# Moving roots, weight splits and a turn in a hybrid encoder trunk

## The chip, the cores and the metric

The kernel runs on one core of one Trainium2 chip. The metric is the device time of one execution in microseconds (us). The engines are named as in the profile: PE is TensorE (matrix products; PEld loads its weights), DVE is VectorE, ACT is ScalarE, POOL is GpSimd, SP issues DMAs.

## The reference

Two token batches (512 and 256 tokens, width 1024, float32) go through a trunk of two layers with shared weights. Each layer is a feed-forward network, a token mixer and a second feed-forward network, each on a normalised input and added to the residual stream:

```python
for li in range(DEPTH):                      # DEPTH = 2
    x = x + 0.5 * swiglu_ffn(rmsnorm(x, norm_g[li, 0]), ffn_w1[li, 0], ffn_w2[li, 0])
    h = rmsnorm(x, norm_g[li, 1])
    mix = hgrn2_mixer(h, ...) if li % 3 == 0 else window_gqa_mixer(h, ...)
    x = x + mix
    x = x + 0.5 * swiglu_ffn(rmsnorm(x, norm_g[li, 2]), ffn_w1[li, 1], ffn_w2[li, 1])
return rmsnorm(x, final_norm_g)
```

The first mixer is a gated linear recurrence in both directions with 8 heads: `f = lb + (1 - lb) * sigmoid(...)` are the gates, the outputs are normalised per head by `rsqrt(mean(o * o) + eps)` and multiplied by `silu(g)`. The second is attention with 16 query heads in 4 groups over a window of 128 tokens on each side, with a rotary turn of 16 of 64 columns, a sink logit per head and a softmax; its output goes through `w_o`.

## The kernel before

Every large product is made of float32 operands that are split in two: a high part (a cast, on ACT) and a low part (the rest, a subtraction on DVE). Three matmuls then replace one: high by high, high by low, low by high (lines 286 to 288, and 524 and 605 in the feed-forward networks, where a seven-product scheme saves one product in eight). Weights come by DMA into four raw buffers, are cast by line 186 and rested by line 187 (227 and 228 in the feed-forward networks) into eight tiles named `w`, in the order of a queue that is planned at the start; a next tile is staged when an earlier one is done with. The 768 tokens stand in six blocks of 128, three to each half.

A feed-forward network ends with six blocks: two residual additions each (line 668), then `after_block`. That normalises the block (`norm_block`: square with its sum on line 344, root on 345, reciprocal on 346, scale on 349). With the third block of a half it defers two "turns": each turn transposes four of the eight 128-column pieces of the half's three blocks on TensorE (line 409), copies them scaled to the high part (416, ACT) and makes the low part (417, DVE). Deferred steps are taken one by one with `run_later`, at places that the loops name. At a mixer both turns of the first half are taken during blocks 4 and 5, those of the second half inside the mixer's first projection, on whose later blocks they bear.

The recurrence projects three outputs per head (a copy and two sigmoids, line 831) and weaves this with the scan of an earlier head. A scan's sections write scores (line 850), multiply running products (943 to 951), copy operands (894, 896), carry a state over the blocks (982, 985) and form the output (998). The sums of squares of the heads' outputs (`hss`) become roots and reciprocals (`hrs`, lines 1066 and 1067) in two batches of four heads; the projection of `g` then uses Silu and multiplies with these (1097 and 1103). ACT has to load a table (ACT_TABLE_LOAD in the profile) when a function of another set is next.

Attention is a pipeline over 24 units of a block and a group. A unit's scores (1383) go through a maximum (1399), exponentials (1412), a sum and its reciprocal (1424, 1425) and a scaling (1428); its weights are transposed (1435), copied (1437) and multiplied with the values (1444). Between units stand pieces of the query projections, whose results are rotated (1158 to 1165), turned (1369) and split (291, 292), and later pieces of the output projection.

The order in which each engine executes is fixed at build time by a scheduling layer that weighs readiness; `issue_after(x)` makes an instruction stand behind instruction `x` in it. Line numbers in the profile are those of the code below; in the changed file they are 2 to 7 higher.

Of the kernel before, what the change touches and what calls it, by code (L numbers as in the profile page):

```python
# [9 lines left out]
F32 = mybir.dt.float32  # L10
# [3 lines left out]
ALU = mybir.AluOpType  # L14
# [35 lines left out]
class Trunk:  # L50
# [125 lines left out]
    def plain_steps(self, key, raw, shape):  # L176
        self.plains += 1
        tiles = []

        def go(part=0, parts=1, eng=self.nc.vector):  # L180
            n = shape[0] * shape[1]
            if not part:
                tiles[:] = [self.wtile()[:, :n].rearrange("p (a b) -> p a b", a=shape[0]) for _ in range(2)]
            ks = slice(part * shape[0] // parts, (part + 1) * shape[0] // parts)
            hi, lo = (t[:, ks, :] for t in tiles)
            self.nc.scalar.copy(hi, raw[:, ks, :])  # L186
            eng.tensor_sub(lo, raw[:, ks, :], hi.bitcast(F32))  # L187
            if part == parts - 1:
                self.staged[key] = (*tiles, 2)

        if self.plains == 1:
            return [(2, lambda: go(0, 2, self.nc.gpsimd)), (0, lambda: go(1, 2, self.nc.gpsimd))]
        if self.plains == 2:
            return [(2, lambda: [go(i, 2) for i in range(2)])]
        return [(2, go)]
# [260 lines left out]

    xn = [None] * NBLK
    normed = mixed = first = halved = None
    plains = 0

    def after_block(self, b, row):
# [208 lines left out]
    def ffn(self, tag, next_row):  # L670
# [59 lines left out]
        for b in range(NBLK):  # L730
            if next_row is None and b == NBLK - 1:
                self.last_block(b, lambda c: [add(b, k, hids[k], (c,)) for k in range(2)] and banks[(b, c)])
                return
            for i, k in (((0, 0), (1, 0), (0, 1)), ((1, 1),))[b] if b < 2 else ((b, 0), (b, 1)):
                add(i, k, hids[k])
            for c in range(2):
                self.added = self.add_x(self.x[b][:, c * 512 : (c + 1) * 512], banks[(b, c)], 0.5)
            self.after_block(b, next_row)
            if b >= 4:
                self.run_later()  # L740

    def spill_x(self):
# [71 lines left out]
    def hgrn_proj(self, h, out):  # L814
        nc = self.nc
        qk = self.big([P, 2, T])
        qs, kd = qk[:, 0, :], qk[:, 1, :]
        f, q, k = (self.big([P, 2, T]) for _ in range(3))
        for c0, dst, func in ((0, qs, AF.Copy), (3, f[:, 1, :], AF.Sigmoid), (4, f[:, 0, :], AF.Sigmoid)):
            key = ("hgrn", h, c0)  # L820
            wh, wl = self.take(key)
            for s, (off, n) in enumerate(SEQS):
                ps = self.ps(n)
                for kk in range(NC):
                    b = tuple(self.h[kk][:, i, off : off + n] for i in range(2))
                    self.mm3(ps, (wh[:, kk, :], wl[:, kk, :]), b, kk == 0, kk == NC - 1)
                    if kk in ((1, 3, 5), (3,))[s]:
                        yield
                if s:
                    self.done(key)  # L830
                nc.scalar.activation(dst[:, off : off + n], ps, func)
                yield
        for d in range(2):
            fd, j = f[:, 1 - d, :], slice(h, h + 1)
            nc.vector.tensor_scalar(fd, fd, self.om_lb[:, d, j], self.lb[:, d, j], ALU.mult, ALU.add)
            nc.scalar.activation(k[:, d, :], fd, AF.Identity, bias=1.0, scale=-1.0)
            nc.vector.tensor_mul(q[:, 1 - d, :], qs, fd)
        nc.vector.tensor_add(kd, k[:, 0, :], k[:, 1, :])
        out.update(h=h, qs=qs, kd=kd, f=f, q=q, k=k)
# [194 lines left out]
    def hgrn(self, lb_row, gn_row, next_row):  # L1034
        nc = self.nc
# [28 lines left out]
        def rstds(half):  # L1064
            r = rs[:, half * 4 : half * 4 + 4, :]
            nc.scalar.activation(r, self.hss[:, half * 4 : half * 4 + 4, :], AF.Sqrt, bias=self.eps, scale=1.0 / P)
            nc.vector.reciprocal(r, r)
# [22 lines left out]
        def put_g(half):  # L1090
            us = {}

            def f(s, b, ps):
                if not half and not us:
                    rstds(0)
                sg = self.tmp(512)
                nc.scalar.activation(sg, ps, AF.Silu)
                off, n = SEQS[s]
# [252 lines left out]
class Unit:  # L1351
# [69 lines left out]
    def denominator(self):  # L1421
        nc = self.k.nc
        den, sk = self.den, self.sk
        nc.vector.tensor_add(den, den, sk)
        nc.vector.reciprocal(den, den)
        for i in range(GQ):
            p = self.sc[:, i, : self.nk]
            nc.vector.tensor_scalar(p, p, den[:, i : i + 1], 1.0, ALU.mult, ALU.mult)

    def probs(self, j):  # L1430
        k = self.k
# [140 lines left out]
```

## Time and profile before

| what | value |
| --- | --- |
| median of 3 runs | 2735.54 us (2735.27 to 2736.42) |
| profiled execution, its time | 2735.33 us |
| its span | 2733.5 us |
| PE busy | 2720.8 us |
| DVE busy | 2111.6 us |
| ACT busy | 1340.6 us |
| POOL busy | 205.0 us |

A row of the timeline gives the start in us from the span's start, the duration in us, the engine, the line, the operation, the tiles written and read, the shapes and a count of merged instructions; in brackets stands how long the engine had been idle before and what released it. Consecutive matmuls overlap: a 512-wide one is shown with 0.39 us, and the next starts 0.23 us after it.

### The profile page before, as it was taken

The numbers are of one execution on the slowest core, as the hardware profiler recorded it, in microseconds if no ns is written. First come the engines' busy times: TensorE is split into PE (matmuls) and PEld (weight loads), VectorE is DVE, ScalarE is ACT, GpSimd is POOL, SyncE is SP. The second block draws the span as 40 slices with busy tenths as digits, with TensorE's granted clock in tenths as the row PEclk, the third lists the DMA queues.
The fourth block names the chain that finished last, engine by engine and source line by source line (L and its number), as shares of the span: only waits on it lengthen the run. The fifth ranks groups of instructions, "written<-read, shape, count | busy, mean of one in ns | idle before, by whom it ended". The sixth has DMA issues, their size and how long they took to land.

```text
span 2733.5 us, 44559 instructions
## 1 busy us (share of the span) xinstructions
PE 2720.8 (100%) x17305; PEld 2483.1 (91%) x17305; DVE 2111.6 (77%) x3789; ACT 1340.6 (49%) x2508; POOL 205.0 (7%) x243
## 2 busy tenths in 40 slices
PE   9999999999999999999999999999999999999998
PEld 9999999889888889999999999999887789999998
DVE  8888788567476778878888878887847768787877
ACT  6444444456466554444446444444446754444444
POOL 1110110000000000011100011101000000111000
PEclk9999999999999999999999999999999999999999
DMA  6554554311110424455543355544512123555443
GB/s 183 137 125 115 127 145 117 123 55 48 55 41 25 141 68 113 120 147 128 128 121 102 89 128 139 135 116 113 147 58 78 47 62 84 133 139 133 118 112 108
DMA packets 331411, 293.98 MB, mean 108 GB/s; under 512 B 11752, under 2 KB 258240, under 8 KB 331200
## 3 DMA queue, kind: packets, MB, share of 16 engines
q1 hardware_dynamic: 294352, 212.89, 26.4%
q0 software_dynamic: 32544, 64.76, 13.3%
q10 hardware_dynamic: 4304, 13.49, 1.4%
q8 instruction: 135, 2.21, 0.3%
q14 instruction: 76, 0.62, 0.1%
HBM read 216.91 MB, written 9.44 MB: 83 GB/s over the span
## 4 chain that ended last, share of the span: by engine, by line
PE 96%; DVE 2%; ACT 1%; issue 0%; DMA 0%; DVEq 0%; SPq 0%; ACTq 0%
PE ps L524 43%; PE ps L605 21%; PE ps L286 8%; PE ps L288 8%; PE ps L287 8%; PE ps L850 1%; PE ps L640 1%; PE ps L998 1%; PE ps L1444 1%; PE ps L1435 1%; PE ps L1383 1%; PE ps L409 1%; PE ps L974 0%; DVE w L187 0%; PE ps L963 0%
## 5 line engine op out<-in xcount | busy, mean ns | idle before, releaser
L524 PE MATMUL ps<-big,w 128*128 128x384 f32 x6720 | 1169.4, 334 | 0.0
L524 PEld LDWEIGHTS ps<-big,w 128*128 128x128 f32 x6720 | 1165.9, 188 | 1.8 <-ACT tA L541 0.2
L227 ACT CAST w<-wr 128x512 fp32r<-128x512 f32 (+1 forms) x606 | 423.6, 710 | 737.7 <-DVE wr L241 327.2
L228 DVE TENSOR_TENSOR w<-wr,w 128x512 fp32r<-128x512 f32 (+1 forms) x606 | 481.2, 799 | 227.7 <-ACT w L227 158.6
L605 PE MATMUL ps<-w,big 128*128 128x512 f32 x2520 | 575.5, 389 | 0.0
L605 PEld LDWEIGHTS ps<-w,big 128*128 128x128 f32 x2520 | 472.6, 188 | 97.8 <-DVE x L668 0.4
L668 DVE SCALAR_TENSOR_TENSOR x<-ps,x 128x512 f32<-128x512 f32 x468 | 303.4, 683 | 8.0 <-PE ps L288 8.0
L286 PE MATMUL ps<-w,big 128*128 128x512 f32 x576 | 232.5, 404 | 0.3
L288 PE MATMUL ps<-w,big 128*128 128x512 f32 x576 | 225.6, 392 | 1.0 <-DVE big L417 1.0
L287 PE MATMUL ps<-w,big 128*128 128x512 f32 x576 | 225.1, 391 | 0.0
L286 PE MATMUL ps<-big,w 128*128 128x384 f32 (+2 forms) x640 | 218.0, 342 | 0.1
L287 PE MATMUL ps<-big,w 128*128 128x384 f32 (+2 forms) x640 | 215.8, 337 | 0.4 <-DVE big L369 0.2
L288 PE MATMUL ps<-big,w 128*128 128x384 f32 (+2 forms) x640 | 215.0, 336 | 0.0
L291 ACT CAST big<-tA 128x384 fp32r<-128x384 f32 x296 | 147.9, 512 | 118.6 <-DVE tA L569 40.4
L153 POOL DMA_DIRECT2D s<-wr x122 | 106.3, 913 | 1300.1 <-DMA wr<-in_ffn_w_dram 614.8
L187 DVE TENSOR_TENSOR w<-wr,w 128x1024 fp32r<-128x1024 f32 (+1 forms) x88 | 106.1, 1210 | 82.5 <-ACT w L186 73.9
L292 DVE TENSOR_TENSOR big<-tA,big 128x384 fp32r<-128x384 f32 x296 | 160.5, 553 | 7.4 <-ACT big L291 7.0
L153 POOL DMA_DIRECT2D wr<-wr x101 | 87.6, 867 | 1010.4 <-DVE tA L1103 387.1
L186 ACT CAST w<-wr 128x1024 fp32r<-128x1024 f32 (+1 forms) x90 | 93.0, 1036 | 91.9 <-PE ps L287 65.6
L286 PEld LDWEIGHTS ps<-w,big 128*128 128x128 f32 x576 | 108.3, 188 | 26.3 <-issue 5.3
L288 PEld LDWEIGHTS ps<-w,big 128*128 128x128 f32 x576 | 108.1, 188 | 25.1 <-DVE big L417 1.7
L287 PEld LDWEIGHTS ps<-big,w 128*128 128x128 f32 x640 | 121.0, 189 | 9.3 <-DVE big L292 1.0
(191 smaller groups left out, 2897.2 us busy)
## 6 DMA issues: line engine op xcount, KB each, us to landing
wr<-in_ffn_w_dram SPq DMA_DIRECT2D x264, 512.0 KB, 3.9
s<-wr POOLq DMA_DIRECT2D x122, 256.0 KB, 5.2
s<-in_ffn_w_dram SPq DMA_DIRECT2D x120, 256.0 KB, 3.3
wr<-wr POOLq DMA_DIRECT2D x80, 256.0 KB, 4.2
wr<-in_hg_w_in_dram SPq DMA_DIRECT2D x40, 512.0 KB, 3.9
wr<-wr POOLq DMA_DIRECT2D x21, 512.0 KB, 6.0
spill<-x ACTq DMA_DIRECT2D x12, 512.0 KB, 3.0
x<-spill ACTq DMA_DIRECT2D x12, 512.0 KB, 3.3
```

Source lines behind the costliest of these rows:

```text
L153: self.nc.gpsimd.dma_start(out, src, accum_op=ALU.add)
L187: eng.tensor_sub(lo, raw[:, ks, :], hi.bitcast(F32))
L227: nc.scalar.copy(h, src)
L228: low = nc.vector.tensor_sub(l, src, h.bitcast(F32)).ins
L286: nc.tensor.matmul(out, a[0], b[0], start=first, stop=False)
L287: nc.tensor.matmul(out, a[0], b[1], start=False, stop=False)
L288: nc.tensor.matmul(out, a[1], b[0], start=False, stop=last)
L291: self.nc.scalar.copy(hi, src)
L292: return self.nc.vector.tensor_sub(lo, src, hi.bitcast(F32)).ins
L524: self.nc.tensor.matmul(ps, a[x], b[y], start=first and k == 0 and i == 0, stop=k == 3 and i == 2, skip_group_check=True,)
L605: nc.tensor.matmul(ps, a[x], w[y], start=name == chain and kp == 0 and q == 0, stop=kp == 1 and q == 2, skip_group_check=True,)
L668: return self.nc.vector.scalar_tensor_tensor(x, ps, c, x, ALU.mult, ALU.add).ins
```

## The change

Three edits. The first batch of the recurrence's roots is ordered behind the last sigmoid: `self.gate` holds the latest sigmoid or copy of a head's projection when the first block of the `g` projection is recorded. The low parts of attention's output weights, all but the first tile's, are ordered behind the latest scaling of a unit that has been recorded (`self.normal`). And where a mixer follows, a deferred step is taken ahead of the norms of blocks 4 and 5 and not behind them.

```diff
@@ -184,7 +184,9 @@
             hi, lo = (t[:, ks, :] for t in tiles)
             self.nc.scalar.copy(hi, raw[:, ks, :])
-            eng.tensor_sub(lo, raw[:, ks, :], hi.bitcast(F32))
+            follow = self.normal if key[0] == "sw_o" and any(key[1:]) else None
+            with self.tc.issue_after(follow) if follow else nullcontext():
+                eng.tensor_sub(lo, raw[:, ks, :], hi.bitcast(F32))
@@ -456,6 +458,7 @@
     normed = mixed = first = halved = None
+    normal = None
@@ -735,8 +738,11 @@
                 self.added = self.add_x(self.x[b][:, c * 512 : (c + 1) * 512], banks[(b, c)], 0.5)
+            mixer = next_row is not None and next_row % 3 == 1
+            if b >= 4 and mixer:
+                self.run_later()
             self.after_block(b, next_row)
-            if b >= 4:
+            if b >= 4 and not mixer:
                 self.run_later()
@@ -828,7 +834,7 @@
-                nc.scalar.activation(dst[:, off : off + n], ps, func)
+                self.gate = nc.scalar.activation(dst[:, off : off + n], ps, func).ins
@@ -1092,7 +1098,8 @@
                 if not half and not us:
-                    rstds(0)
+                    with self.tc.issue_after(self.gate):
+                        rstds(0)
@@ -1425,7 +1432,7 @@
             p = self.sc[:, i, : self.nk]
-            nc.vector.tensor_scalar(p, p, den[:, i : i + 1], 1.0, ALU.mult, ALU.mult)
+            self.k.normal = nc.vector.tensor_scalar(p, p, den[:, i : i + 1], 1.0, ALU.mult, ALU.mult).ins
```

How the orders change, at the places of which the prediction speaks. First ACT, in the scans of head 3 (before) and head 7 (behind the last sigmoid; `big_8244` and `big_8595` are its scores and transposed keys). Before, in head 3:

```order
L894 COPY big_7296<-big_6444 128x768
L1066 ACT_TABLE_LOAD
L1066 ACTIVATE hrs<-hss,eps 128x24
L896 COPY big_6441<-big_6443 128x768
L894 COPY big_6441<-big_6444 128x768
L894 COPY big_7296<-big_6444 128x768
L831 ACT_TABLE_LOAD
L831 ACTIVATE big_7180<-ps_7353 128x512
```

And of the change, in head 7:

```order
L837 ACTIVATE big_8044<-ps_8478 128x256
L1072 ACT_TABLE_LOAD
L1072 ACTIVATE hrs<-hss,eps 128x24
L886 COPY big_8244<-ps_8542 64x6x64
L842 ACTIVATE big_8046<-big_8044 128x768
L886 COPY big_8244<-ps_8541 64x6x64 x2
L970 COPY big_8595<-ps_8596 128x512
L970 COPY big_8595<-ps_8602 128x512
L886 COPY big_8244<-ps_8542 64x6x64
L892 COPY big_8244<-big_8246 32x6x32 x4
L900 COPY big_8703<-big_8046 128x768
L1104 ACT_TABLE_LOAD
```

Both loads are gone from head 3; one load and the roots stand behind the last sigmoid, and one copy for the next scan has moved behind the four copies of scores.

Second DVE, at the first mixer's start (at the second it is alike): `w_4667` and `w_4676` are the low parts of the projection's third and fourth weight tiles. Before:

```order
L668 SCALAR_TENSOR_TENSOR x_131<-ps_4659,x_131 128x512
L346 RECIPROCAL stat_4618<-stat_4618 128x1
L417 SCALAR_TENSOR_TENSOR big_4623<-ps_4631,cols,big_4623 128x384
L349 TENSOR_SCALAR big_4617<-x_129,stat_4618 128x1024
L417 SCALAR_TENSOR_TENSOR big_4624<-ps_4637,cols,big_4624 128x384
L417 SCALAR_TENSOR_TENSOR big_4625<-ps_4643,cols,big_4625 128x384
L417 SCALAR_TENSOR_TENSOR big_4626<-ps_4649,cols,big_4626 128x384
L187 TENSOR_TENSOR w_4667<-wr_4407,w_4666 128x1024
L417 SCALAR_TENSOR_TENSOR big_4627<-ps_4689,cols,big_4627 128x384
L187 TENSOR_TENSOR w_4676<-wr_4439,w_4675 128x1024
L346 RECIPROCAL stat_4684<-stat_4684 128x1
L417 SCALAR_TENSOR_TENSOR big_4628<-ps_4695,cols,big_4628 128x384
```

Of the change:

```order
L419 SCALAR_TENSOR_TENSOR big_4620<-ps_4643,cols,big_4620 128x384
L671 SCALAR_TENSOR_TENSOR x_131<-ps_4655,x_131 128x512
L671 SCALAR_TENSOR_TENSOR x_131<-ps_4659,x_131 128x512
L348 RECIPROCAL stat_4650<-stat_4650 128x1
L189 TENSOR_TENSOR w_4667<-wr_4407,w_4666 128x1024
L351 TENSOR_SCALAR big_4649<-x_129,stat_4650 128x1024
L189 TENSOR_TENSOR w_4676<-wr_4439,w_4675 128x1024
L419 SCALAR_TENSOR_TENSOR big_4621<-ps_4683,cols,big_4621 128x384
L419 SCALAR_TENSOR_TENSOR big_4622<-ps_4689,cols,big_4622 128x384
L419 SCALAR_TENSOR_TENSOR big_4623<-ps_4695,cols,big_4623 128x384
L419 SCALAR_TENSOR_TENSOR big_4624<-ps_4701,cols,big_4624 128x384
L348 RECIPROCAL stat_4708<-stat_4708 128x1
```

The first turn's low parts (the last of four is the first row) now precede block 5's additions, and the second turn's four stand together behind both splits and ahead of block 5's reciprocal (the last row) and scale.

Third DVE, in attention at the first two of the output weights' late splits: `w_20580` and `w_20643` are their low parts, `big_20503` and `big_20591` two successive units' scores. Before:

```order
L1425 RECIPROCAL stat_20505<-stat_20505 128x4
L187 TENSOR_TENSOR w_20580<-wr_19627,w_20579 128x1024
L1428 TENSOR_SCALAR big_20503<-big_20503,stat_20505 128x384 x4
L292 TENSOR_TENSOR tA_20588<-ps_20585,tA_20588 128x256
L1399 ISA big_20591,stat_20592<-ps_20598,big_18930,nsinks 128x384
L1399 ISA stat_20592 128x1
L292 TENSOR_TENSOR big_20621<-ps_20599,big_20620 128x2x128
L1418 TENSOR_TENSOR stat_20594<-stat_20592,nsinks 128x4
L187 TENSOR_TENSOR w_20643<-wr_19646,w_20642 128x1024
```

Of the change:

```order
L1432 RECIPROCAL stat_20505<-stat_20505 128x4
L1406 ISA big_20591,stat_20592<-ps_20598,big_18930,nsinks 128x384
L1406 ISA stat_20592 128x1
L1435 TENSOR_SCALAR big_20503<-big_20503,stat_20505 128x384 x4
L189 TENSOR_TENSOR w_20580<-wr_19627,w_20579 128x1024
L294 TENSOR_TENSOR tA_20588<-ps_20585,tA_20588 128x256
L294 TENSOR_TENSOR big_20621<-ps_20599,big_20620 128x2x128
L1425 TENSOR_TENSOR stat_20594<-stat_20592,nsinks 128x4
```

The first late split has changed sides with the scaling and the fourth maximum, and the second has left this stretch: it stands behind the next unit's scaling, with the third right behind it. On PE the eight transposes that wait for the scaling, four of which stood between the first two matmuls of a group and four behind the second, now stand together ahead of that group.

## The prediction

> **What bounds the kernel now.** I read the page's busy shares and its chain first, then the list of what TensorE waited for, then the timeline at each such wait.
>
> ```profile
> span 2733.5 us, 44559 instructions
> PE 2720.8 (100%) x17305; PEld 2483.1 (91%) x17305; DVE 2111.6 (77%) x3789; ACT 1340.6 (49%) x2508; POOL 205.0 (7%) x243
> PE 96%; DVE 2%; ACT 1%; issue 0%; DMA 0%; DVEq 0%; SPq 0%; ACTq 0%
> ```
>
> TensorE (PE) is busy for 2720.8 of 2733.5 us and makes 96% of the chain that ended last. So whatever the change does to VectorE (DVE) and ScalarE (ACT), time can only come from moments at which TensorE itself stands still. Its list of waits is short. It counts from the modelled end of a matmul; the loss is read better from start to start. The first place is in the recurrence, head 3:
>
> ```profile
> 750.80 1.28 ACT L1066 ACT_TABLE_LOAD   x1
> 752.10 0.32 ACT L1066 ACTIVATE hrs<-hss,eps 128x24 f32<-128x24 f32 x1
> 755.32 0.39 PE L288 MATMUL ps<-big,w 128*128 128x512 f32 x1
> 756.03 1.28 ACT L831 ACT_TABLE_LOAD   x1
> 757.33 0.60 ACT L831 ACTIVATE big<-ps 128x512 f32<-128x512 f32 x1
> 757.82 0.83 ACT L896 COPY big<-big 128x768 f32<-128x768 f32 x1
> 758.68 0.96 DVE L951 TENSOR_TENSOR big<-big,big 128x768 f32<-128x768 f32 x1 [1.60 <-ACT big L896]
> 758.18 0.28 PE L287 MATMUL ps<-big,w 128*128 128x256 f32 x1
> 758.30 0.28 PE L288 MATMUL ps<-big,w 128*128 128x256 f32 x1
> 759.69 1.48 PE L850 MATMUL ps<-big,big 128*32 128x32 f32 x144 [1.11 <-DVE big L951]
> ```
>
> Matmuls of this width start every 0.12 us (758.18 to 758.30), and the next one starts 1.39 later: lost 1.27. The chain behind it is the table load for the sigmoid (756.03), the sigmoid, the copy L896, the product L951, the scores L850. The sigmoid's table has to be loaded again because the roots at 752.10 had put theirs in its place.
>
> The second and third are the first projections of the two mixers:
>
> ```profile
> 506.98 0.27 PE L409 MATMUL ps<-ident_r,big 128*128 128x128 f32 x1
> 507.75 0.50 PE L288 MATMUL ps<-w,big 128*128 128x512 f32 x1 [0.50 <-DVE big L417]
> 1980.93 0.27 PE L409 MATMUL ps<-ident_r,big 128*128 128x128 f32 x1
> 1981.66 0.50 PE L288 MATMUL ps<-w,big 128*128 128x512 f32 x1 [0.46 <-DVE big L417]
> ```
>
> A transpose takes 0.11 of TensorE's time (four in 0.45, 2132.04 to 2132.49 below), so 0.77 and 0.73 between these starts are losses of 0.66 and 0.62. The matmul waits for the low part of the turned input (L417), which on DVE stands behind a split of a weight tile (L187).
>
> The fourth and fifth are in attention, where the splits of the output weights begin:
>
> ```profile
> 2129.27 0.17 DVE L1425 RECIPROCAL stat<-stat 128x4 f32<-128x4 f32 x1
> 2129.59 1.23 DVE L187 TENSOR_TENSOR w<-wr,w 128x1024 fp32r<-128x1024 f32 x1
> 2130.73 1.40 DVE L1428 TENSOR_SCALAR big<-big,stat 128x384 f32<-128x384 f32 x4
> 2132.38 0.61 DVE L1399 CUSTOM_DVE_ANT_0 big<-ps,big,nsinks 128x384 f32<-128x384 f32 x1
> 2130.31 0.40 PE L286 MATMUL ps<-w,big 128*128 128x512 f32 x1
> 2131.29 0.68 PE L1435 MATMUL ps<-ident_r,big 128*128 128x128 f32 x4 [0.58 <-DVE big L1428]
> 2132.04 0.69 PE L1435 MATMUL ps<-ident_r,big 128*128 128x128 f32 x4
> 2132.49 0.48 PE L288 MATMUL ps<-w,big 128*128 128x512 f32 x1
> 2136.07 1.04 ACT L186 CAST w<-wr 128x1024 fp32r<-128x1024 f32 x1
> 2137.38 0.59 ACT L1437 COPY tA<-ps 128x512 f32<-128x512 f32 x1
> 2137.42 0.40 PE L288 MATMUL ps<-w,big 128*128 128x512 f32 x1
> 2138.02 0.65 PE L1444 MATMUL ps<-tA,big 128*64 128x256 f32 x4 [0.20 <-ACT tA L1437]
> ```
>
> A 512-wide matmul occupies TensorE for 0.23, so the transposes lose 0.98 - 0.23 = 0.75 to the split that stands ahead of L1428, and L1444 loses 0.60 - 0.23 = 0.37 to a copy that stands behind a cast. The five together are 1.27 + 0.66 + 0.62 + 0.75 + 0.37 = 3.67 us, 0.13% of the run: the ceiling of what this change can give.
>
> **The change part by part. Roots.** In the new order ACT has 18 table loads for 19 and none in head 3. The 512-wide product that the sigmoid reads ends at 755.32 + 0.39 = 755.7, so the sigmoid runs from about 755.75, not 757.33, the copy from 756.25 to 757.05 and L951 (0.96) to 758.05. TensorE is there at 758.42. The 1.27 goes, with 0.3 of cover.
>
> The load and the roots now stand in head 7, between the last sigmoid and the copies of the scores:
>
> ```profile
> 842.69 0.38 ACT L831 ACTIVATE big<-ps 128x256 f32<-128x256 f32 x1
> 844.15 0.96 ACT L880 COPY big<-ps 64x384 f32<-64x384 f32 x2 [1.09 <-PE ps L850]
> 853.50 1.12 DVE L985 SCALAR_TENSOR_TENSOR big<-big,big,ps 128x128 f32<-128x128 f32 x4
> 854.80 0.38 PE L998 MATMUL ps<-x,big 128*128 128x128 f32 x2
> ```
>
> ACT idles from 843.07 to 844.15. Load and roots take 1.62 together (750.80 to 752.42), with the usual overlap of 0.1 some 1.5, so L880 starts 0.45 late. From there ACT has no gap up to the Silu's load; the copies that the states need follow that, L985 follows these, and its end at 854.62 is 0.18 ahead of L998. There is no other cover: I take 0.35 lost, near the row's count, with bounds of 0 (the slack in these handovers swallows it) and 1.5 (none of the idle time serves). The reciprocal of the roots moves along to a place where DVE has time ahead of its users.
>
> By its neighbouring rows a load costs 1.30 on ACT: the roots start 0.02 after its end. The Trainium skill (ScalarE: Activation LUTs, What ACT_TABLE_LOAD costs) adds a drain of about 1.38 to each switch, 2.66 in all; by that the new place would lose 1.4 more and the time be 2734.1. This trace shows no such gap at these loads.
>
> **Mixers.** The first turn's four scaled copies (L416) and low parts (L417) now come ahead of the squares and scales of blocks 4 and 5, and the second turn's low parts stand in a row behind both splits. I lay the new order out with the rows' durations:
>
> ```profile
> 496.53 1.47 PE L409 MATMUL ps<-ident_r,big 128*128 128x128 f32 x12
> 498.71 0.56 ACT L416 ACTIVATE big<-ps,cols 128x384 fp32r<-128x384 f32 x1
> 500.75 1.06 ACT L186 CAST w<-wr 128x1024 fp32r<-128x1024 f32 x1
> 501.69 1.08 ACT L344 ACTIVATE big<-x 128x1024 f32<-128x1024 f32 x1
> ```
>
> The first turn's transposes start at 496.53, so the copies run from 497.05 to 499.15, block 4's square to 500.2, the casts end at 501.3 and 503.5, and block 5's square at 505.6. On DVE four L417 end at 500.5, the splits at 503.1 and 504.7, the second turn's L417 at 505.2, 505.7, 506.2 and 506.8, and block 5's scale at 507.8. TensorE needs the first of these at 506.1, the others 0.7 to 0.9 apart, and block 5 at about 509. Nothing is late by this count: both stalls, 1.28, go. What comes late next is block 5's norm, with 1.2 of cover; each us beyond costs one per mixer. Bounds: 0 and 1.28 gained. On ACT's DMA queue the spills of blocks 2 and 3 and the load of the masks (of the rotary and band tables in attention) change places with these; the buffers that the spills free are written by the copies that follow each projected block, the third some 20 us later, and the masks wait for the scan. SP's weight loads wait for the splits, which end earlier.
>
> **Output weights.** Four of the late splits move: the one at 2129.59 behind L1428, the next two together behind the following unit's L1428, and one more later in the same way. DVE then runs the fourth L1399 (0.61) from 2129.37 and L1428 from 2130.0. But TensorE's order moves too: all eight transposes now stand together at 2130.31, and their pace is DVE's, 0.33 for each quarter. The last scaled quarter ends at 2131.4, TensorE follows 0.15 later, and the eight are done at 2131.77: 1.46 for 0.88 of work, 0.58 lost. Before, 2130.31 to 2132.49 held two matmuls and the eight, 0.46 + 0.88, with 0.84 lost. So 0.26 is gained here. The copy ahead of L1444 loses the cast in front of it and what precedes it comes 0.7 earlier, while two of the four L1444 move 0.9 forward: 0.3 of the 0.37. Together 0.55; bounds 0 and 1.12. The splits' users are far off: the first of these weights is read at 2139, the others when the second column half begins.
>
> **Sum.** -1.27 + 0.35 - 1.28 - 0.55 = -2.75 on the profiled run's 2735.33 (1.8 around its span) gives 2732.6; the median of the three runs is 0.2 above that run, so I say 2732.7, 0.1% less.
>
> **The rivals.** *Half comes back.* A TensorE that arrives earlier meets the next tight place, block 5's norm or L998, sooner. For it: DVE is busy for 77% of the span and for more in these stretches. Against it: outside the five places TensorE's list has little. If the mixers give half and attention nothing, -1.27 + 0.35 - 0.64 = -1.56; if head 7 loses its 1.5 and the rest goes as counted, -1.6: 2733.9 both ways.
>
> *Slower: attention's exponentials come late.* In the new ACT order the next unit's four exponentials (L1412) stand behind three copies of transposed weights instead of ahead of them:
>
> ```profile
> 2138.23 0.52 ACT L1412 ACTIVATE big<-big,stat 128x256 f32<-128x256 f32 x1
> 2141.55 1.14 DVE L1428 TENSOR_SCALAR big<-big,stat 128x256 f32<-128x256 f32 x4
> 2146.91 1.03 PE L1435 MATMUL ps<-ident_r,big 128*128 128x128 f32 x8
> ```
>
> They begin at about 2141.4, 3.2 late. TensorE wants their result at 2146.91, and it was ready at 2142.69: cover of 4.2. If a split that waits on DVE for its cast (1.23) and the reordered L1399 (0.6 each) use that up, lateness goes straight to TensorE; from 6.4 us late the 2.2 gained elsewhere is lost. With all 3.2 uncovered the sum is -1.27 + 0.35 - 1.28 + 3.2 = +1.0: 2736.5.
>
> *It does nothing.* The five losses only change their place: 2735.5. Against it: head 3's loads are gone from the order.
>
> *All of it.* No loss in head 7 and both attention losses gone, -3.67: 2731.9.
>
> **How the numbers follow.** Chances: forecast 0.62, half back 0.20, all of it 0.08, nothing 0.06, slower 0.04. The range 2731.5 to 2735.0 holds the first three and leaves out the last two and some scatter, under 2 in 10. About 0.2% (5.5 us) is what a measurement of this kernel can tell from no change; the ceiling of 3.67 lies below it, and so does the slower rival's 1.0. So within 0.2% has 0.96, and each side keeps 0.02 for something that no row here shows.
>
> **What would show it.** Right: no table load near 751 and 756, and L850 at about 758.4 less what the first mixer gave; no wait of L288 behind the transposes in either mixer; at the first late split some 0.6 lost at L1435 and no wait at L1444; a new wait of 0.3 to 0.4 at L998 in head 7. Wrong: a wait of L409 on block 5's scale, of L1435 on L1428 one unit later, or a loss above 1 us at L998.

## The result, and the profile after

| what | before | after |
| --- | --- | --- |
| median, 20 runs of each | 2735.78 us (2735.27 to 2737.84) | 2732.43 us (2731.37 to 2733.40) |
| profiled execution, its time | 2735.33 us | 2732.59 us |
| its span | 2733.5 us | 2730.5 us |

The ratio is 0.9987 with a 95% interval of 0.9981 to 0.9993: 3.35 us less. That is a gain, and smaller than the 0.2% that the prediction took as the least that can be told. The forecast was 2732.7.

Two lines of the page of the changed kernel, the busy times and the chain:

```profile
PE 2720.2 (100%) x17305; PEld 2483.8 (91%) x17305; DVE 2110.3 (77%) x3789; ACT 1339.0 (49%) x2507; POOL 204.8 (7%) x243
PE 97%; DVE 1%; ACT 1%; issue 0%; DMA 0%; DVEq 0%; SPq 0%; ACTq 0%
```

TensorE has the same 17305 matmuls and makes 97% of the chain for 96%. ACT has one instruction less. What TensorE waited for (us in total, times, the longest):

```profile
PE ps L104 <- DVE eps L101: 1.1, 1, 1.1
PE ps L527 <- ACT tA L544: 0.6, 1, 0.6
PE ps L362 <- DVE big L351: 0.5, 1, 0.5
PE ps L1004 <- DVE big L991: 0.3, 1, 0.3
PE ps L289 <- DVE big L371: 0.2, 1, 0.2
```

The waits for scores, for the turned inputs and in attention are gone. The line of L1004 (L998 before) is not new: the list of the kernel before has the same 0.3, there at 892.79 and here at 891.22, in the output of the last scan, 38 us behind that of head 7. What the roots cost in head 7 is not in this list. L527 stands in the first feed-forward network, where the two programs are the same. It is a loss of this one execution, as the last experiment shows.

Head 3 of the changed kernel, ACT and then TensorE (start, duration, engine, line; in brackets the idle time before). What is called head 3 in this document is the stretch behind that head's output, where its scores L850 are already those of the next scan; what is called head 7 is the stretch beside head 7's projection, and its L998 forms the output of the scan before the last one:

```profile
755.28 0.60 ACT L837 ACTIVATE big<-ps 128x512 f32<-128x512 f32 x1 [0.98 <-PE ps L290]
758.04 1.48 PE L856 MATMUL ps<-big,big 128*32 128x32 f32 x144
```

No table load is left, the sigmoid follows its product, and the scores L856 wait for nothing. In head 7:

```profile
841.38 1.28 ACT L1072 ACT_TABLE_LOAD   x1
842.90 0.46 ACT L886 COPY big<-ps 64x384 f32<-64x384 f32 x1
852.21 1.12 DVE L991 SCALAR_TENSOR_TENSOR big<-big,big,ps 128x128 f32<-128x128 f32 x4
853.11 0.38 PE L1004 MATMUL ps<-x,big 128*128 128x128 f32 x2
```

The copies start 0.42 late (TensorE stands 1.67 earlier here than in the kernel before, and 844.15 - 1.67 = 842.48), and L991 ends at 853.33, 0.22 behind the start of the first L1004. The next rows of L1004 start at 853.38 and 853.71, after 0.27 and 0.33; in the kernel before it was 0.22 and 0.23 (854.80, 855.02, 855.25). So 0.15 is lost, too little for the list.

At the first mixer, these are the kernel before and then the changed one:

```profile
500.12 1.38 DVE L668 SCALAR_TENSOR_TENSOR x<-ps,x 128x512 f32<-128x512 f32 x2 [1.64 <-PE ps L288]
500.60 1.49 PE L409 MATMUL ps<-ident_r,big 128*128 128x128 f32 x12
501.48 0.60 DVE L417 SCALAR_TENSOR_TENSOR big<-ps,cols,big 128x384 fp32r<-128x384 f32 x1
502.22 0.47 PE L286 MATMUL ps<-w,big 128*128 128x512 f32 x1
```

```profile
499.22 2.18 DVE L419 SCALAR_TENSOR_TENSOR big<-ps,cols,big 128x384 fp32r<-128x384 f32 x4
501.43 1.47 PE L411 MATMUL ps<-ident_r,big 128*128 128x128 f32 x12
502.66 0.48 PE L288 MATMUL ps<-w,big 128*128 128x512 f32 x1
505.51 2.18 DVE L419 SCALAR_TENSOR_TENSOR big<-ps,cols,big 128x384 fp32r<-128x384 f32 x4
507.80 0.75 DVE L351 TENSOR_SCALAR big<-x,stat 128x1024 f32<-128x1024 f32 x1
509.39 0.60 PE L411 MATMUL ps<-ident_r,big 128*128 128x128 f32 x4
```

From the twelve transposes to the first matmul of the projection it was 1.62 before and is 1.23 now. Before, that matmul began only 0.14 after the end of the first low part L417 (502.08), which stood on DVE behind block 5's additions (L668). DVE had been idle for 1.64 ahead of these; in the changed kernel the first turn's four low parts (L419 at 499.22) use that time, and all that is behind them on DVE moves up. The prediction had not listed this loss of 0.39. (The profile names the weight cast L186 as what the load of this matmul waited for. But the cast had ended at 501.81, and PE's queue passed its semaphore for L286 only at 502.12, right behind the end of L417. Why a product of two high parts waits for a low part was not explored; both parts stand in one tile.) The four low parts of the second turn (L419) now stand in a row from 505.51, block 5's norm is done at 508.55, and its transposes at 509.39 do not wait.

In attention, at the first late split and one unit later:

```profile
2126.57 0.17 DVE L1432 RECIPROCAL stat<-stat 128x4 f32<-128x4 f32 x1
2127.17 1.41 DVE L1435 TENSOR_SCALAR big<-big,stat 128x384 f32<-128x384 f32 x4
2127.74 1.44 PE L1442 MATMUL ps<-ident_r,big 128*128 128x128 f32 x8
2132.88 0.58 ACT L1444 COPY tA<-ps 128x512 f32<-128x512 f32 x1
2133.42 0.40 PE L289 MATMUL ps<-w,big 128*128 128x512 f32 x1
2133.75 0.65 PE L1451 MATMUL ps<-tA,big 128*64 128x256 f32 x4
```

The scaling follows the reciprocal without a split between them; only the next unit's fourth maximum stands there. The eight transposes take 1.44, where eight elsewhere take 1.04 (2143.60 below). L1451 starts 0.33 after the matmul ahead of it and loses 0.1, for 0.37 before.

**Where the time went.** The table gives, for each kernel, how the start times of its matmuls moved against the same matmuls of the kernel before, both counted from the first matmul of the profiled execution. Each column is the step at one place (the difference of the medians behind and ahead of it, us); steps under 0.1 are left out. The kernels from "roots" on are the experiments below.

```
                     first FFN  mixer 1        head 3  head 7  mixer 2        attention            whole
                     (chance)   L286   L288                    L286   L288    split  L1444  later
changed                +0.83   -0.38  -0.85   -1.16   +0.12   -0.40  -0.70   -0.40  -0.21  +0.17   -2.91
changed, again           .     -0.38  -0.85   -1.16   +0.13   -0.40  -0.71   -0.39  -0.21  +0.16   -3.83
roots                  +0.17     .      .     -1.16   +0.14     .      .     +0.28    .      .     -0.79
mixers                 +0.12   -0.38  -0.85     .       .     -0.40  -0.70   +0.29    .      .     -1.93
weights                +0.14     .      .       .       .       .      .     -0.39  -0.21  +0.20   -0.30
fourth maximum         +0.11   -0.38  -0.86   -1.14   +0.17   -0.41  -0.70   -0.59    .    +0.16   -3.77
first turn only          .     -0.38  -0.83     .       .     -0.40  -0.75     .      .      .     -2.43
second turn only       -0.11     .      .       .       .       .      .     +0.29    .      .      0.00
roots behind head 5      .       .    -0.10   -1.16     .       .      .       .      .      .     -0.93
one load more, head 7    .       .      .     -1.16   +1.41     .      .       .      .      .     -0.15
reload alone             .       .      .     -0.91   +0.17     .      .       .      .      .     -0.73
changed, head 5          .     -0.38  -0.85   -1.14     .     -0.41  -0.70   -0.11  -0.22  +0.17   -3.60
```

Steps elsewhere, in the feed-forward networks, come and go by up to 0.3 (one of +0.32 in the kernel with the roots behind head 5). The whole runs over the last column's matmuls and holds these too. The changes of the medians, each against the kernel before on the same chip, point the same way: roots 2735.30 for 2736.12, mixers 2734.12, weights 2735.89; first turn 2733.47 for 2735.77, second turn 2736.23. But the interval of the ratio reaches 1 in each of the experiments 1 to 3 and 5 to 9, so it is the steps and not the times that carry the argument there.

### The profile page after: what moved, and what is told of

Read it like the earlier page. It is cut to its first block, busy times and chain, and to the rows that moved or that the text cites. A ratio compares the mean times of both kernels' runs of the same rounds, so it can differ in the third digit from the quotient of the medians.

```text
span 2730.5 us, 44549 instructions
## 1 busy us (share of the span) xinstructions
PE 2720.2 (100%) x17305; PEld 2483.8 (91%) x17305; DVE 2110.3 (77%) x3789; ACT 1339.0 (49%) x2507; POOL 204.8 (7%) x243
## 4 chain that ended last, share of the span: by engine, by line
PE 97%; DVE 1%; ACT 1%; issue 0%; DMA 0%; DVEq 0%; SPq 0%; ACTq 0%
PE ps L527 42%; PE ps L608 21%; PE ps L288 9%; PE ps L289 9%; PE ps L290 9%; PE ps L856 1%; PE ps L643 1%; PE ps L1451 1%; PE ps L1442 1%; PE ps L1004 1%; PE ps L1390 1%; PE ps L411 1%; PE ps L980 0%; PE ps L969 0%; DVE x L671 0%
## 5 line engine op out<-in xcount | busy, mean ns | idle before, releaser
L527 PE MATMUL ps<-big,w 128*128 128x384 f32 x6720 | 1169.7, 334 | 0.6 <-ACT tA L544 0.6
L527 PEld LDWEIGHTS ps<-big,w 128*128 128x128 f32 x6720 | 1165.9, 188 | 2.8 <-ACT tA L544 1.2
L288 PE MATMUL ps<-w,big 128*128 128x512 f32 x576 | 232.5, 404 | 0.0
L288 PE MATMUL ps<-big,w 128*128 128x384 f32 (+2 forms) x640 | 217.9, 342 | 0.2
L186 ACT CAST w<-wr 128x1024 fp32r<-128x1024 f32 (+1 forms) x90 | 93.0, 1035 | 93.4 <-PE ps L289 66.3
L288 PEld LDWEIGHTS ps<-w,big 128*128 128x128 f32 x576 | 108.3, 188 | 25.6 <-issue 4.6
```

The source lines that it names most:

```text
L288: nc.tensor.matmul(out, a[0], b[0], start=first, stop=False)
L527: self.nc.tensor.matmul(ps, a[x], b[y], start=first and k == 0 and i == 0, stop=k == 3 and i == 2, skip_group_check=True,)
```

## The experiments

**1. The roots' edit alone.**

```diff
-                nc.scalar.activation(dst[:, off : off + n], ps, func)
+                self.gate = nc.scalar.activation(dst[:, off : off + n], ps, func).ins
...
-                    rstds(0)
+                    with self.tc.issue_after(self.gate):
+                        rstds(0)
```

> The kernel before with the roots' edit alone. Read by the difference between the start times of the same matmuls in this run and in the one before. The prediction's count: -1.27 in head 3 and +0.35 in head 7, -0.9 together. The reading of the two traces: -1.2 and +0.17, -1.05. The rival by which the loss only changes its place: 0 together, with a new wait in a later head. The other three losses stay where they were: 0.66 and 0.62 at L288 in the mixers, 0.75 and 0.37 in attention. Its time against the kernel before: 0.9996 in each of the first two cases, 1.0 in the third.

Measured: -1.16 in head 3 and +0.14 in head 7, -1.02 together; ratio 0.9998 (0.9989 to 1.0007). The reading of the traces holds, and the prediction's 0.35 for head 7 was too much. The waits at the mixers and in attention stayed. The step of +0.28 in attention, in a place that this edit doesn't touch, is taken up under the hardware.

**2. The mixers' edit alone.**

```diff
+            mixer = next_row is not None and next_row % 3 == 1
+            if b >= 4 and mixer:
+                self.run_later()
             self.after_block(b, next_row)
-            if b >= 4:
+            if b >= 4 and not mixer:
                 self.run_later()
```

> The kernel before with the mixers' edit alone. The prediction's count: only the waits of L288 behind the transposes go, -0.66 and -0.62, -1.28 together, and the start of the projection's first L286 behind the twelve transposes stays at 1.62 from these. The reading of the two traces: that L286 also waited for the first low part of the turned input, so 0.39 more goes in each mixer: 1.23 in place of 1.62, and -1.2 and -1.15 in the two mixers, -2.35 together. The rival by which half comes back: -0.64 together, with a wait on block 5's scale. Ratios 0.9995, 0.9991 and 0.9998.

Measured: -0.38 and -0.85 at the first mixer, -0.40 and -0.70 at the second: -2.33 together, the reading of the traces and not the prediction's -1.28. Ratio 0.9993 (0.9984 to 1.0002).

**3. The edit of the output weights alone.**

```diff
+            follow = self.normal if key[0] == "sw_o" and any(key[1:]) else None
+            with self.tc.issue_after(follow) if follow else nullcontext():
+                eng.tensor_sub(lo, raw[:, ks, :], hi.bitcast(F32))
...
+            self.k.normal = nc.vector.tensor_scalar(p, p, den[:, i : i + 1], 1.0, ALU.mult, ALU.mult).ins
```

> The kernel before with the edit of the output weights alone. The prediction's count: -0.26 at the transposes of the first late split, which then run at the pace of the scaling with 0.58 lost, and -0.3 at L1444, -0.55 together. The reading of the two traces: -0.6 together, 0.5 lost at the transposes, and +0.15 some units later. The rival by which the exponentials come late: a new wait of the transposes in a following unit, up to +1.0. The other losses of the kernel before stay: 1.27 in head 3, 0.66 and 0.62 at the mixers. Ratio 0.9998, too near to 1 for the times to tell.

Measured: -0.39 at the transposes, -0.21 at L1444, +0.20 later: -0.40 together; ratio 0.9999 (0.9990 to 1.0008). No wait of the transposes a unit later. With the two runs ahead this adds up to -1.02 - 2.33 - 0.40 = -3.75, and the changed kernel, run again, has -3.81 in the same columns. By these steps the three edits do not disturb each other.

The +0.2 is akin to the slower rival, by another way: exponentials that come late hold up a copy. ACT's order in the changed kernel at that place, and the products that wait:

```profile
2173.42 0.59 ACT L1444 COPY tA<-ps 128x512 f32<-128x512 f32 x1 [1.24 <-PE ps L1442]
2176.62 0.56 ACT L1444 COPY tA<-ps 128x512 f32<-128x512 f32 x1
2176.21 1.69 PE L1451 MATMUL ps<-tA,big 128*64 128x256 f32 x12
```

Before, the twelve products took 1.52. Now four exponentials stand behind the copy at 2173.42, which waits 1.24 for its transposes, so the last copy comes only at 2176.62, when the products have begun. All five kernels with this edit show the step, none of the others.

**4. The fourth maximum behind the scaling.** On the changed kernel:

```diff
+            hold = i == GQ - 1 and k.normal is not None
+            with k.tc.issue_after(k.normal) if hold else nullcontext():
                 nc.vector.tensor_tensor_reduce(
...
```

> The changed kernel, and the fourth maximum of each unit is ordered behind the latest scaling recorded. By its order this moves two instructions: at the first late split the next unit's fourth maximum (0.54 of DVE's time) now stands behind the scaling and not ahead of it, and the same one unit later. If the maximum ahead of the scaling is what makes the eight transposes run at DVE's pace, their row falls from 1.44 to about 0.95 and 0.5 goes: -0.5 against the changed kernel. If the exponentials' chain is as tight behind it, the next unit's transposes lose what this one gains: 0. If the scaling waits for something else (the denominator's chain from ACT), the row stays at 1.44: 0.

The rows at the first late split:

```profile
2126.04 0.17 DVE L1434 RECIPROCAL stat<-stat 128x4 f32<-128x4 f32 x1
2126.24 1.41 DVE L1437 TENSOR_SCALAR big<-big,stat 128x384 f32<-128x384 f32 x4
2127.08 1.39 PE L1444 MATMUL ps<-ident_r,big 128*128 128x128 f32 x8
```

The scaling starts 0.20 after the reciprocal and not 0.60, and 0.84 ahead of the transposes for 0.57. Yet their row only falls from 1.44 to 1.39; besides, it starts 0.23 behind the matmul ahead of it and not 0.35 (2127.39 to 2127.74). The step at the split is -0.59 for -0.39, and most of it is missing again at the products one unit later (under 0.1 for -0.21). The second expectation is the nearest: 0.2 was gained, not 0.5, and 0.14 of it was lost again. 2732.14 us (ratio 0.9985, 0.9976 to 0.9994) is the changed kernel's time within what can be told.

**5 and 6. One turn at a time.** On the kernel before, only block 4's deferred step ahead of the norm, and then only block 5's (`b == 5`):

```diff
+            if b == 4 and mixer:
+                self.run_later()
             self.after_block(b, next_row)
-            if b >= 4:
+            if b >= 4 and not (b == 4 and mixer):
                 self.run_later()
```

> The kernel before, and at a mixer only block 4's deferred step (the first half's first turn) stands ahead of that block's norm; block 5's stays behind. The first four low parts are then made some 2 us sooner, with both weight splits moving up behind them, and the second turn's low parts stand with block 5's norm among them as before. Theory of the missed loss: L286 behind the transposes starts at 1.23 from these and not 1.62, and most of the wait at L288 goes too, since the splits come sooner: -1.0 in each mixer, at least -0.8. Rival, each turn carries its own loss: -0.39 for this turn, and the wait of 0.66 and 0.62 at L288 stays. The prediction's count, that L288's wait is the whole loss and needs both turns: 0 to -0.66.

> The kernel before, and at a mixer only block 5's deferred step (the second turn) stands ahead of that block's norm. The first turn's low parts and the splits stay as late as before, so the second low part of this turn, for which L288 waits, ends at about 507.6 for 507.7 before. Theory: 1.62 at L286 stays, L288's wait shrinks by 0.1 only, so -0.1 in each mixer. Rival, each turn carries its own loss: -0.66 and -0.62, with L286 at 1.62. If block 5's norm now comes late, a wait of L409 on its scale shows, up to +0.5.

The first turn alone, then the second alone:

```profile
500.60 1.47 PE L409 MATMUL ps<-ident_r,big 128*128 128x128 f32 x12
501.82 0.48 PE L286 MATMUL ps<-w,big 128*128 128x512 f32 x1
```

```profile
500.49 1.50 PE L409 MATMUL ps<-ident_r,big 128*128 128x128 f32 x12
502.11 0.47 PE L286 MATMUL ps<-w,big 128*128 128x512 f32 x1
507.69 0.50 PE L288 MATMUL ps<-w,big 128*128 128x512 f32 x1 [0.52 <-DVE big L417]
```

The first turn has everything: 1.22 to L286, -1.21 in the first mixer and -1.15 in the second, as much as both together (-1.23 and -1.10). The second has nothing: 1.62 to L286 and the wait at L288 as before. So both waits have one cause, the first turn's low parts, which stood on DVE behind block 5's additions and around block 4's norm, with the weight splits behind them. The rival by which each turn carries its own loss falls. The second turn's new place neither helps nor harms.

**7. The roots one place earlier.** The roots' edit on the kernel before, with the gates of head 6 and 7 not recorded, so that the roots stand behind head 5's last and the sigmoid's table is loaded again for head 6:

```diff
-                self.gate = nc.scalar.activation(dst[:, off : off + n], ps, func).ins
+                act = nc.scalar.activation(dst[:, off : off + n], ps, func).ins
+                if h <= 5:
+                    self.gate = act
```

> The kernel before with the roots behind the last gate of head 5 in place of head 7, so that the sigmoid's table has to be loaded again, ahead of head 6's last sigmoid: 19 loads. If the load ahead of a sigmoid is what loses time (the prediction's chain of load, sigmoid, copy, product, scores), the loss of 1.27 goes from head 3 and comes back in head 6 at the scores, with 0.1 to 0.4 at L998 for the load behind the gate: +0.2 to +0.4 against the kernel before. If it is the roots' place in head 3 that matters (they stood late there, behind the copies), the loss goes and does not come back: -1.0. If each switch of tables drains ACT by another 1.38 us, the load behind the gate loses 1.4 more: +1.6.

```profile
790.76 1.28 ACT L831 ACT_TABLE_LOAD   x1
792.05 0.60 ACT L831 ACTIVATE big<-ps 128x512 f32<-128x512 f32 x1
794.47 1.48 PE L852 MATMUL ps<-big,big 128*32 128x32 f32 x144
```

-1.16 in head 3, and it does not come back: as many loads as before, one of them again straight ahead of a sigmoid, and no step in head 5, 6 or 7. ACT had nothing to do from 790.74 on; the load needs no data, so it ran while the product was still being made, and the sigmoid was some 0.35 late in place of 1.6. The prediction's chain in head 3 (load, sigmoid, copy, product, scores) is a true list of what happened there. But a load ahead of a sigmoid does not by itself lose the time.

**8. One load more in head 7.** The roots' edit alone, and behind the roots a sigmoid into a scratch tile that nothing reads (the line that makes the tile `junk` is left out):

```diff
                     with self.tc.issue_after(self.gate):
                         rstds(0)
+                        nc.scalar.activation(self.junk, self.hss[:, 0:4, :], AF.Sigmoid)
```

> The roots' edit alone, and behind the roots in head 7 one more sigmoid of 24 columns into a scratch tile that nothing reads, so that a second load stands there (19 loads in all). It measures the cover in head 7. One load there cost 0.17 by the two traces. If its cover was used up, the second costs its whole 1.28 plus the small sigmoid, 1.4 to 1.6 more at L998 or the scores' copies: +0.5 against the kernel before, -1.2 in head 3 and +1.6 to +1.8 in head 7. If the copies it delays had time left, less: 0.5 more would say that the cover of a load there is about 1. With a drain of 1.38 at each switch: 2.9 more.

```profile
842.93 0.32 ACT L1067 ACTIVATE hrs<-hss,eps 128x24 f32<-128x24 f32 x1
843.26 1.28 ACT L1098 ACT_TABLE_LOAD   x1
844.56 0.22 ACT L1098 ACTIVATE junk<-hss 128x24 f32<-128x24 f32 x1
844.69 0.83 ACT L836 ACTIVATE big<-big 128x768 f32<-128x768 f32 x1
```

+1.41 in head 7, 1.27 more than with one load, where 1.4 to 1.6 more was expected. The second pair keeps ACT for 1.43 (843.26 to 844.69), so nearly all of it reaches TensorE: the first load and the roots have used up what ACT had idle there. Three loads stand in 9.4 us here, and each begins within 0.03 of the end of what is ahead of it and is followed as closely: no drain.

**9. The reload alone in head 3.** The roots' edit, and a root of a scratch tile behind head 5's first output, so that the sigmoid at 756 has its load again but the roots do not come back (the lines that make the tile are left out):

```diff
+                if h == 5 and c0 == 0 and s:
+                    with self.tc.issue_after(self.gate):
+                        nc.scalar.activation(self.junk, self.junk, AF.Sqrt)
```

> The roots' edit alone, and in head 5's projection (the one beside head 3's scan) one root of 24 columns of a scratch tile behind the copied output, so that the sigmoid's table has to be loaded again ahead of the same sigmoid as in the kernel before, at about 756, while the roots and their load stay away from 750.80. 20 loads in all. If the reload ahead of the sigmoid is by itself what loses 1.27 in head 3 (the prediction's chain), the loss is back: step of 0 there against the kernel before. If it was the sum of both loads and the roots between two gaps of ACT (1.62 + 1.30 against gaps of 1.2 and 1.0), the reload fits into what ACT has idle: the sigmoid starts at about 756.1 and not 757.33, and -1.2 stays gained, at most 0.1 less. With 0.12 to 0.17 lost in head 7 as in the run with the roots' edit alone.

```profile
754.18 0.83 ACT L899 COPY big<-big 128x768 f32<-128x768 f32 x1 [1.09 <-DVE big L948]
755.03 1.28 ACT L833 ACT_TABLE_LOAD   x1
756.33 0.60 ACT L833 ACTIVATE big<-ps 128x512 f32<-128x512 f32 x1
758.69 1.48 PE L855 MATMUL ps<-big,big 128*32 128x32 f32 x144 [0.18 <-DVE big L956]
```

Two loads more than with the roots' edit alone, one at 747.04 and this one, cost 0.25 (-0.91 for -1.16); 0.1 was expected. These are the copy and the sigmoid with the roots' edit alone (experiment 1):

```profile
753.99 0.84 ACT L894 COPY big<-big 128x768 f32<-128x768 f32 x1 [1.19 <-DVE big L943]
755.79 0.60 ACT L831 ACTIVATE big<-ps 128x512 f32<-128x512 f32 x1 [0.97 <-PE ps L288]
```

So the loss of the kernel before was a sum. The load and the roots at 750.80 made this copy 1.19 late (755.18); the gap ahead of it could not take that up, since it is a wait for DVE's product of an earlier copy, and moves along. Only then did the second load find the gap ahead of the sigmoid too short: 1.19 + 1.30 - 0.97 = 1.52, and the sigmoid was 1.54 late (757.33 for 755.79). In experiment 9 TensorE stands 0.11 earlier here than in experiment 1 (755.26 for 755.37 at the sigmoid's last product), so the load added at 747.04 made the copy 0.30 late and the sigmoid came 0.65 late, which cost 0.25: the scores have cover for some 0.4. The reload alone would make the sigmoid 0.33 late (1.30 - 0.97), and the first load and the roots alone 0.22 (1.19 - 0.97); by this estimate neither would cost anything by itself.

**10 and 11. The changed kernel with the roots behind head 5, and the changed kernel again.** The edit of experiment 7 on the changed kernel, and no edit.

> The changed kernel with the roots behind head 5's last gate in place of head 7's, one load more. By the run with that place on the kernel before, the load behind head 5's gate and the reload in head 6 lose nothing that shows, while head 7's place lost 0.12 to 0.17: -0.15 against the changed kernel by the steps of the matmul starts, which the times cannot tell. If loads add up somewhere, +0.2 or more. In the first feed-forward network, where the program is the same as before, the loss of 0.66 at 472.6 in the profiled execution of the changed kernel should not be there if it was chance.

> The changed kernel once more. If the 0.66 at 472.6 (and 0.2 near 2699) of its first profiled execution was chance, its TensorE starts differ there as in the six other runs, -0.2 against the kernel before, and its sum of steps is -3.8, about 0.9 below the first one's -2.9. If the loss belongs to the program, +0.66 is there again.

The cost in head 7 is gone with the roots behind head 5, as expected. The whole is 0.2 less all the same, since this execution's step at the split is -0.11, for a reason that the last section shows. The time is 2731.93 us for 2731.99 of the changed kernel again (ratios 0.9987, 0.9978 to 0.9996, and 0.9988, 0.9978 to 0.9998): nothing that can be told apart. The second execution of the changed kernel has no wait at L527 and no step in the first network; the +0.83 of the first was chance, from a cause that is open. Its whole is -3.83.

## Why the prediction was right, and where it was wrong

**What bounds it.** Right: all of the gain came from moments at which TensorE stood still. DVE's and ACT's busy times hardly moved.

**Roots, head 3.** The size was right (1.16 for 1.27), the scores come at 758.04 without a wait, and there is cover left. The cause was named too narrowly: not the sigmoid's load but two loads and the roots in one stretch (experiments 7 and 9). Taking the roots away and keeping the reload gives 0.91 of the 1.16, with a load at 747.04 in their stead; taking only the reload away was not tried.

**Roots, head 7.** 0.35 was put in, 0.12 to 0.17 was measured. The delays were counted rightly: L991's end moved back by 0.38, where 0.45 was counted, against the cover of 0.18 that the prediction had read. Its own rows gave 0.2 to 0.27, and the choice went above that. Nor did the sign come that it named, a wait of 0.3 to 0.4 at L998 in head 7: the loss is too small for the list of waits. The drain of 1.38 that the Trainium skill adds to a load (ScalarE: Activation LUTs, What ACT_TABLE_LOAD costs) does not appear: with it, experiment 8 would have cost 2.9 more, and it cost 1.27.

**Mixers.** This is the term that failed: 1.28 counted, 2.33 measured, from 0.66 and 0.62 to 1.23 and 1.10. The prediction read the losses from the list of waits and from the starts around L288. The wait of the first L286 behind twelve transposes is not in that list, since a modelled end covers it. At 0.11 each, twelve transposes take 1.32; 1.62 between the starts left 0.3 to be explained, and the row of L417 that ends at 502.08 was in reach. This loss of 0.39, once in each mixer, makes 0.78 of the missing 1.05. Of the rest, 0.1 in each mixer is that the matmul behind the one that waited starts 0.33 and not 0.23 after it (507.75 to 508.08, 1981.66 to 1981.99); the last 0.1, in the first mixer, is not traced. The prediction's layout of the new order held: the second turn's low parts in a row, block 5's norm next, and no wait of L411 on it. By experiment 5 the first turn alone brings the whole gain.

**Output weights.** 0.55 counted, 0.44 measured in the changed kernel (0.40 + 0.21 - 0.17). At the split 0.26 was counted and 0.40 came; at L1444 0.3 and 0.21. What the count left out is the 0.17 given back at 2176.

**The rivals.** The slower one was no phantom. In the first unit behind the split the exponentials came even later than it said:

```profile
2138.84 0.52 ACT L1419 ACTIVATE big<-big,stat 128x256 f32<-128x256 f32 x1
2142.11 1.13 DVE L1435 TENSOR_SCALAR big<-big,stat 128x256 f32<-128x256 f32 x4
2143.60 1.04 PE L1442 MATMUL ps<-ident_r,big 128*128 128x128 f32 x8
```

Against the kernel before, TensorE stands 3.3 earlier here, so 2138.84 is 3.9 late (2138.23 - 3.3 = 2134.9). The scaled weights are ready at 2143.24, 0.36 ahead of the transposes: of the cover of 4.2 nearly all is used up, and nothing is lost. Later, at 2176, late exponentials held up a copy that had no such cover, and it cost 0.17. "Half comes back" and "nothing" are out. "All of it" was held to 3.67, the sum of the five losses that the list showed. That was called a ceiling and was none: the change gave 3.8 in the undisturbed execution, since two losses of 0.39 were not in the sum.

**The time.** 2732.7 was close, but for the wrong reason. The profiled time fell by 2.74, almost the sum of 2.75; yet the change itself gave 3.8 there, and 0.83 was lost by chance in the first network and 0.26 near the end (at 2699), where the second execution lost nothing. Over many runs the gain is 3.35 (20 runs of each) and 3.56 (10 and 25 runs), 0.6 to 0.8 more than the sum. The mixers' missing 1.05 is more than that, and head 7 lost 0.2 less than counted; the 3.8 of the steps lies within the interval of the ratio (1.9 to 5.2 us less).

## What to carry to other kernels

Read the starts around every change of the kind of work on the busy engine, not only its list of waits: a wait that ends inside a modelled end is not listed, and here two such waits held a fifth of the gain (0.78 of 3.8). When an engine that executes in order makes another late, look for what lies ahead of it up to its last gap, and try which part alone suffices; the last instruction ahead of the late one need not be the one that costs. And when a step is moved, keep what was left of its new cover: 0.36 was left here, and the next edit in that place may be the one that pays.

## What the runs showed of the hardware that was not expected

A table load waits for no data. In every execution here each load but the program's first starts within 0.02 of the end of what is ahead of it on ACT, so in a gap ahead of a function it costs 1.30 less the gap: 0.35 late in head 6 (experiment 7), and nothing on TensorE.

One handover had two lengths. Two units ahead of the late split a copy follows eight transposes; these are the rows of the kernel with the roots' edit, and then of the changed kernel:

```profile
2116.60 1.03 PE L1436 MATMUL ps<-ident_r,big 128*128 128x128 f32 x8
2117.57 0.59 ACT L1438 COPY tA<-ps 128x512 f32<-128x512 f32 x1 [1.97 <-PE ps L1436]
```

```profile
2114.96 1.03 PE L1442 MATMUL ps<-ident_r,big 128*128 128x128 f32 x8
2115.65 0.59 ACT L1444 COPY tA<-ps 128x512 f32<-128x512 f32 x1 [1.69 <-PE ps L1442]
```

The copy began 0.97 or 0.69 after the row's start, 0.28 apart, in programs that are alike there. Four of the thirteen executions had the longer one, and they are the four whose step at the split is 0.28 or so worse than that of their like in the table (roots, mixers, second turn, and the changed kernel with head 5). What decides it is open. A step of 0.3 between two single executions is therefore no finding by itself in this kernel.
